# Eight weight tiles made 32 bytes longer in a hybrid decoder layer

## The chip, the cores and the metric

The kernel runs on one core of a Trainium2 chip. The metric is the device time of one execution in microseconds; the median of three executions before the change is 2016.8 us.

## What is computed

One decoder layer over 256 tokens of width 2048, all in float32: a feed-forward block (SwiGLU, inner width 5632), a mixer, a second feed-forward block, and a last RMS norm. Cut to what matters here:

```python
x = x + 0.5 * _swiglu(_rmsnorm(x, n1), w_gate1, w_up1, w_down1)
x = x + _mixer(_rmsnorm(x, nm), ...)      # h @ w_in (2048 x 8208), retention and gated delta heads, mixed @ w_out
x = x + 0.5 * _swiglu(_rmsnorm(x, n2), w_gate2, w_up2, w_down2)
return _rmsnorm(x, nf)
```

The weights (some 376 MB) are each used once, for all 256 tokens.

## The kernel before

**A product.** Every large product keeps the tokens as the stationary operand (a 128 x 128 piece of the activations, loaded into TensorE) and streams the weights as the moving operand, 128 x 512 at a time, into a PSUM accumulator for 128 tokens x 512 output columns. To keep float32 accuracy each operand is split into a high and a low part in the type float32r, and three matmuls are made of each pair (`triple`, lines 149 to 151): high activations with high weights (`whi`), high activations with low weights (`wlo`), low activations with high weights. The three come back to back, so while one matmul streams, the stationary operand of the next one is loaded (the rows called PEld).

**The weights' way.** `weight_piece` (lines 128 to 137) brings one piece, two blocks of 128 rows x 512 columns, so 4096 bytes on each of the 128 partitions: SyncE issues a DMA into `raw` (line 131), ScalarE rounds it into `whi` (line 135), VectorE writes the rest into `wlo` (line 136). A piece then serves 12 matmuls (2 row blocks, 2 token tiles, 3 matmuls). `Stream.take` asks for pieces some places ahead in a plan written out beforehand. The pool `wraw` has four buffers of `raw`; the pool `wsp` has four of `whi` and four of `wlo`, which are used in turn. Only the last four pieces of the whole program go to another pool, `pools["last"]`, which the change leaves as it is. The piece `wab` of the mixer's gates brings its own tile.

**The stages and their stationary operands**, in order of time. The last column counts the matmuls of lines 149 to 151.

| stage | product | stationary tiles | matmuls |
|---|---|---|---|
| first feed-forward | gate and up | `xh`, `xl` | 2112 |
| first feed-forward | down | `hh`, `hl` | 1056 |
| mixer | input, `w_in` | `xh`, `xl` | 1536 |
| mixer | output, `w_out` | `mh..`, `ml..`, `m8` | 384 |
| second feed-forward | gate and up | `xh`, `xl` | 2112 |
| second feed-forward | down | `hh`, `hl` | 1056 |

Each feed-forward block runs in two halves, gate and up of a half and then down of that half, so its two rows of the table alternate. In the mixer the matmuls of `w_in` are interleaved, by a count written in the code (`advance`, one step for each matmul triple), with the steps of the head computations.

**Where the tiles lie.** Tiles stand one behind the other in each partition. An address here is the place of a tile's first byte in its partition, as the built program has it, modulo 256 bytes. A row block of a stationary tile begins a multiple of 512 bytes behind the tile's start, the second row block of a weight piece 2048 bytes behind the first, so the address of a whole tile modulo 256 is that of each operand in it.

| tiles | before | after |
|---|---|---|
| `whi` of `wsp`, buffers 0 to 3 | 160, 160, 160, 160 | 160, 192, 224, 0 |
| `wlo` of `wsp`, buffers 0 to 3 | 160, 160, 160, 160 | 32, 64, 96, 128 |
| `whi`, `wlo` of the last four pieces | 160 | 160 |
| `raw` | 160 | 160 |
| `xh`, `xl` | 160 | 160 |
| `hh`, `hl` in the first feed-forward block | 0 | 0 |
| `hh`, `hl` in the second feed-forward block | 160 | 160 |
| `mh..`, `ml..`, `m8` | 0 | 0 |
| `gu` (moving) and `slr` (stationary) of line 735, in the mixer | 0 and 224 | 0 and 224 |

The distance of two addresses, below, is the moving operand's less that of the stationary operand which is loaded while it streams, modulo 256. Before, it is 0 in every stage whose stationary tiles are at 160, and 160 in the first block's down product and in `w_out`.

Of the kernel before, what the change touches and what calls it, by code (L numbers as in the profile page):

```python
# [14 lines left out]
F32R = mybir.dt.float32r  # L15
# [4 lines left out]
P = 128  # L20
# [5 lines left out]
NB = 512  # L26
# [61 lines left out]
def hybrid_layer(ctx: ExitStack, tc: tile.TileContext, a: dict, out: bass.AP):  # L88
# [8 lines left out]
    wsp = ctx.enter_context(tc.tile_pool(name="wsp", bufs=4))  # L97
# [30 lines left out]
    def weight_piece(src, k, n, pool=wsp, both=None):  # L128

        raw = wraw.tile([P, k, n], F32, name="raw")  # L130
        nc.sync.dma_start(raw, src)
        if both is None:
            both = pool.tile([P, k, n], F32R, name="whi"), pool.tile([P, k, n], F32R, name="wlo")
        hi, lo = both
        S.copy(hi, raw)  # L135
        V.tensor_tensor(lo, raw, hi.bitcast(F32), ALU.subtract)  # L136
        return hi, lo
# [24 lines left out]
    class Stream:  # L162
# [9 lines left out]
        def take(self, w, n):  # L172
            while self.at < len(self.plan) and len(self.ready) <= self.lead:
                name, src, k, pool = self.plan[self.at]
                self.ready.append((name, k, weight_piece(src, k, NB, pools[pool] if pool else wsp)))
                self.at += 1
            name, k, parts = self.ready.popleft()
            assert (name, k) == (w, n)
            return parts
# [289 lines left out]
    with tc.tile_pool(name="gd", bufs=1) as gd:  # L469
        def mixed_out(o, b, xt=None):  # L470
            for t in range(NT):
                xs = x[:, t, b * NB:(b + 1) * NB]
                V.tensor_tensor(xs, o[t], xs, ALU.add)
            later.extend(norm_block(ssqs[2], 2, b, xt))

        env = dict(x_left=x_left, ident=ident, mx=mx, product=product, product_units=product_units, power=power,
                   vector_transposed=vector_transposed, split=split,
                   weight_piece=weight_piece, do_later=do_later, mixed_out=mixed_out,
                   row_factor=lambda: row_factor(ssqs[1]), params=(cst, alog, dtb, gnw, cw, posi))
        mixer(tc, a, gd, env)  # L480
# [605 lines left out]
```

## Time and profile before

| | |
|---|---|
| median of three runs | 2016.8 us (2014.28 to 2017.02) |
| the profiled execution's own time | 2015.32 us |
| its span, first to last instruction | 2013.5 us |
| mean granted TensorE clock | 0.993 of full speed |
| TensorE busy with matmuls | 98% of the span |
| VectorE, ScalarE, GpSimd busy | 65%, 44%, 4% |
| mean busy share of the DMA engines, by slice | mostly 0.5 to 0.6 |

How to read it: the matmuls are pipelined, and a row's duration reaches from a matmul's start to its modelled end, which lies behind the start of the next. So busy time says little on the rate; the distance between the starts of two matmuls that follow each other does, here called the spacing. In a window full of equal matmuls it is the window's length plus one duration, divided by the count (a window counts each matmul that touches it).

### The profile page before, as it was taken

Reading aid. Unit: us, or ns where it says so; the run is one execution under the profiler, and the core shown is the slowest. Engines: PE = TensorE matmul, PEld = TensorE weight load, DVE = VectorE, ACT = ScalarE, POOL = GpSimd, SP = SyncE. Lnnn points to the kernel's source line nnn. Section 1 sums busy time; section 2 is a strip of 40 time slices with the busy share of each in tenths; the row PEclk is TensorE's granted clock in tenths of the full one; section 3 lists DMA queues with packets and bytes.
Section 4 is the critical chain, followed back from the end, with each engine's and each line's share of the span. In section 5 each row is a group of like instructions: output and inputs, shape, how many; then the busy total and the mean of one; then the engine's idle time right before and its main releaser. Section 6 shows DMA issues by size and latency. Waiting matters only on the chain.

```text
span 2013.5 us, 23688 instructions
## 1 busy us (share of the span) xinstructions
PE 1974.1 (98%) x8804; PEld 1617.5 (80%) x8804; DVE 1315.8 (65%) x1878; ACT 890.9 (44%) x1076; POOL 86.9 (4%) x121
## 2 busy tenths in 40 slices
PE   9999999999999999998998999999999999999998
PEld 7888888888888888866877778888888888888886
DVE  6776664457666766564896697766676554667654
ACT  6434443343444446633643344444444434444443
POOL 0000000000000000220132100000000000000000
PEclk9999999999999999998998999999999999999999
DMA  8655655565565566797468555666665556655564
GB/s 302 202 185 188 208 190 188 188 191 186 188 208 189 183 188 181 153 207 161 145 180 200 124 158 184 215 192 194 194 193 187 200 195 192 195 192 188 184 208 142
DMA packets 197604, 379.91 MB, mean 189 GB/s; under 512 B 15280, under 2 KB 15920, under 8 KB 197360
## 3 DMA queue, kind: packets, MB, share of 16 engines
q1 hardware_dynamic: 193888, 368.40, 59.5%
q0 software_dynamic: 3168, 8.65, 1.7%
q8 instruction: 69, 1.13, 0.2%
q10 hardware_dynamic: 432, 1.34, 0.2%
q14 instruction: 47, 0.39, 0.1%
HBM read 375.98 MB, written 2.36 MB: 188 GB/s over the span
## 4 chain that ended last, share of the span: by engine, by line
PE 85%; DVE 5%; DMA 4%; issue 4%; POOL 1%; ACT 1%; DVEq 0%; POOLq 0%; ACTq 0%
PE acc L149 28%; PE acc L151 27%; PE acc L150 27%; DMA nr<-nd 2%; DVE wlo L136 2%; DMA raw<-in_w_in_dram 1%; PE mx L791 1%; DVE mt L254 0%; PE mx L713 0%; DMA nd<-Nd 0%; DVE yn L825 0%; ACT whi L135 0%; DVE Yd L826 0%; POOL nr L810 0%; DVE ht L254 0%
## 5 line engine op out<-in xcount | busy, mean ns | idle before, releaser
L136 DVE TENSOR_TENSOR wlo<-raw,whi 128x1024 fp32r<-128x1024 f32 (+1 forms) x689 | 838.7, 1225 | 557.4 <-ACT whi L135 554.4
L135 ACT CAST whi<-raw 128x1024 fp32r<-128x1024 f32 (+1 forms) x689 | 719.3, 1050 | 859.4 <-PE acc L151 738.6
L149 PE MATMUL acc<-whi,xh 128*128 128x512 f32 x1920 | 760.5, 396 | 1.4 <-DVE xl L269 1.3
L150 PE MATMUL acc<-wlo,xh 128*128 128x512 f32 x1920 | 751.5, 391 | 6.7 <-DVE wlo L136 6.7
L151 PE MATMUL acc<-whi,xl 128*128 128x512 f32 x1920 | 750.8, 391 | 0.0
L150 PEld LDWEIGHTS acc<-wlo,xh 128*128 128x128 f32 x1920 | 362.1, 189 | 81.7 <-DVE wlo L136 10.8
L149 PEld LDWEIGHTS acc<-whi,xh 128*128 128x128 f32 x1920 | 362.1, 189 | 75.7 <-ACT whi L135 3.4
L151 PEld LDWEIGHTS acc<-whi,xl 128*128 128x128 f32 x1920 | 361.8, 188 | 75.4
L149 PE MATMUL acc<-whi,hh 128*128 128x512 f32 x704 | 276.5, 393 | 0.0
L150 PE MATMUL acc<-wlo,hh 128*128 128x512 f32 x704 | 276.5, 393 | 0.0
L151 PE MATMUL acc<-whi,hl 128*128 128x512 f32 x704 | 276.5, 393 | 0.0
L254 DVE STREAM_TRANSPOSE ht<-h 32x256 f32<-32x256 f32 x352 | 153.3, 436 | 5.3
L150 PEld LDWEIGHTS acc<-wlo,hh 128*128 128x128 f32 x704 | 132.4, 188 | 30.0
L151 PEld LDWEIGHTS acc<-whi,hl 128*128 128x128 f32 x704 | 132.4, 188 | 29.9
L149 PEld LDWEIGHTS acc<-whi,hh 128*128 128x128 f32 x704 | 132.4, 188 | 29.8
L141 ACT CAST hh<-ht 128x512 fp32r<-128x512 f32 x44 | 27.2, 618 | 121.3 <-DVE ht L254 121.3
L298 POOL TENSOR_TENSOR rfac<-rms,cexpn 128x2 f32<-128x2 f32 (+1 forms) x5 | 3.2, 642 | 866.0 <-DVE rms L304 866.0
L142 DVE TENSOR_TENSOR hl<-ht,hh 128x512 fp32r<-128x512 f32 x44 | 30.3, 688 | 14.5 <-ACT hh L141 14.4
L345 ACT ACTIVATE sg<-acc,rfac 128x512 f32<-128x512 f32 x44 | 29.9, 689 | 20.2 <-PE acc L151 17.4
L149 PE MATMUL acc<-whi,mh 128*128 128x512 f32 x96 | 38.1, 396 | 0.0
L151 PE MATMUL acc<-whi,ml 128*128 128x512 f32 x96 | 38.1, 396 | 0.0
L150 PE MATMUL acc<-wlo,mh 128*128 128x512 f32 x96 | 38.0, 396 | 0.0
(205 smaller groups left out, 843.8 us busy)
## 6 DMA issues: line engine op xcount, KB each, us to landing
raw<-in_ffn_w_up_dram SPq DMA_DIRECT2D x176, 512.0 KB, 4.4
raw<-in_ffn_w_down_dram SPq DMA_DIRECT2D x176, 512.0 KB, 4.4
raw<-in_ffn_w_gate_dram SPq DMA_DIRECT2D x175, 512.0 KB, 4.4
raw<-in_w_in_dram SPq DMA_DIRECT2D x128, 512.0 KB, 4.8
raw<-in_w_out_dram SPq DMA_DIRECT2D x32, 512.0 KB, 4.3
nr<-nd POOLq DMA_DIRECT2D x64, 128.0 KB, 7.7
x<-in_x_dram SPq DMA_DIRECT2D x4, 512.0 KB, 6.8
out_dram<-x SPq DMA_DIRECT2D x8, 256.0 KB, 2.4
```

The lines of the kernel that those rows point to most:

```text
L135: S.copy(hi, raw)
L136: V.tensor_tensor(lo, raw, hi.bitcast(F32), ALU.subtract)
L141: S.copy(hi, src)
L142: V.tensor_tensor(lo, src, hi.bitcast(F32), ALU.subtract)
L149: PE.matmul(o, lhsT=sh, rhs=hi, start=first, stop=False)
L150: PE.matmul(o, lhsT=sh, rhs=lo, start=False, stop=False)
L151: PE.matmul(o, lhsT=sl, rhs=hi, start=False, stop=last)
L254: V.transpose(dv[q:q + Q, :, :, r:r + Q], sv[r:r + Q, :, :, q:q + Q])
L298: G.tensor_tensor(dst, src, cexp[e][:, 0:1].broadcast_to([P, w]), ALU.pow)
L345: S.activation(sg[:, t, :], g[t], AF.Silu, scale=rf[:, t:t + 1])
L791: PE.matmul(pt[:m, i, :], lhsT=lhsT, rhs=rhs, start=True, stop=True)
```

## The change

Each of the eight tiles of the pool `wsp` gets 8 more float32 elements behind its 1024, which no instruction reads or writes. So each tile begins 32 bytes further on, modulo 256, than the one before it. Eight times 32 is 256, so all tiles behind the pool move by 256 bytes and keep their addresses modulo 256. Line numbers behind the change grow by two. The instructions, their engines, their order, their sizes, buffers and waits stay the same on all five queues; only the addresses in them differ.

```diff
         if both is None:
-            both = pool.tile([P, k, n], F32R, name="whi"), pool.tile([P, k, n], F32R, name="wlo")
+
+            both = [pool.tile([P, 2 * NB + (8 if pool is wsp else 0)], F32R, name=name)[:, :k * n]
+                    .rearrange("p (k n) -> p k n", n=n) for name in ("whi", "wlo")]
         hi, lo = both
```

## Rows read from the trace of the kernel before

**Rows 1.** The page's head and its busy time by engine.
```profile
span 2013.5 us, 23688 instructions
...
PE 1974.1 (98%) x8804; PEld 1617.5 (80%) x8804; DVE 1315.8 (65%) x1878; ACT 890.9 (44%) x1076; POOL 86.9 (4%) x121
```

**Rows 2.** The page's chain of work that ended last, by engine and line.
```profile
PE 85%; DVE 5%; DMA 4%; issue 4%; POOL 1%; ACT 1%; DVEq 0%; POOLq 0%; ACTq 0%
PE acc L149 28%; PE acc L151 27%; PE acc L150 27%; DMA nr<-nd 2%; DVE wlo L136 2%; DMA raw<-in_w_in_dram 1%; PE mx L791 1%; DVE mt L254 0%; PE mx L713 0%; DMA nd<-Nd 0%; DVE yn L825 0%; ACT whi L135 0%; DVE Yd L826 0%; POOL nr L810 0%; DVE ht L254 0%
```

**Rows 3.** The page's costliest groups: busy us, mean ns, idle before.
```profile
L136 DVE TENSOR_TENSOR wlo<-raw,whi 128x1024 fp32r<-128x1024 f32 (+1 forms) x689 | 838.7, 1225 | 557.4 <-ACT whi L135 554.4
L135 ACT CAST whi<-raw 128x1024 fp32r<-128x1024 f32 (+1 forms) x689 | 719.3, 1050 | 859.4 <-PE acc L151 738.6
L149 PE MATMUL acc<-whi,xh 128*128 128x512 f32 x1920 | 760.5, 396 | 1.4 <-DVE xl L269 1.3
...
L150 PE MATMUL acc<-wlo,xh 128*128 128x512 f32 x1920 | 751.5, 391 | 6.7 <-DVE wlo L136 6.7
...
L149 PE MATMUL acc<-whi,hh 128*128 128x512 f32 x704 | 276.5, 393 | 0.0
```

**Rows 4.** Windows of single stages: length, busy us and count by engine.
```profile
core 0: us, PE busy (x) PEld busy (x) DVE busy (x) ACT busy (x) POOL busy (x), PEclk, DMA share, GB/s
...
60.00:270.00 210.00, 209.24 (x923) 172.84 (x922) 139.16 (x176) 92.04 (x99) 0.00 (x0) 1.00 0.62 196
280.00:400.00 120.00, 120.00 (x514) 96.48 (x513) 59.65 (x56) 46.39 (x46) 0.00 (x0) 1.00 0.56 188
405.00:620.00 215.00, 215.00 (x950) 178.00 (x949) 134.83 (x161) 92.89 (x97) 0.00 (x0) 1.00 0.61 193
...
740.00:1190.00 450.00, 423.92 (x2025) 345.15 (x2024) 309.17 (x604) 207.41 (x303) 82.16 (x110) 0.97 0.68 166
1200.00:1280.00 80.00, 80.00 (x343) 64.33 (x342) 67.03 (x105) 36.46 (x49) 0.00 (x0) 1.00 0.54 184
...
1600.00:1700.00 100.00, 100.00 (x443) 82.81 (x442) 48.92 (x43) 39.08 (x38) 0.00 (x0) 1.00 0.59 195
```

**Rows 5.** Groups by line, windows 280 to 400 and 1290 to 2000 us.
```profile
L149 PE MATMUL acc<-whi,hh 128*128 128x512 f32 x171 | 67.8, 396 | 0.0
...
L149 PE MATMUL acc<-whi,hh 128*128 128x512 f32 x346 | 134.6, 389 | 0.0
```

**Rows 6.** Timeline of PE behind the first down product: start us, duration us.
```profile
404.88 0.39 PE L151 MATMUL acc<-whi,hl 128*128 128x512 f32 x1
...
406.96 0.39 PE L151 MATMUL acc<-whi,xl 128*128 128x512 f32 x1
```

**Rows 7.** Timeline of PE behind a late weight load, gate and up.
```profile
54.54 0.39 PE L151 MATMUL acc<-whi,xl 128*128 128x512 f32 x1
...
56.62 0.39 PE L151 MATMUL acc<-whi,xl 128*128 128x512 f32 x1
```

**Rows 8.** Timeline of PE around two matmuls of line 735, mixer.
```profile
996.48 0.39 PE L149 MATMUL acc<-whi,xh 128*128 128x512 f32 x1
996.71 0.62 PE L735 MATMUL mx<-gu,slr 128*128 128x512 f32 x2
997.17 0.39 PE L150 MATMUL acc<-wlo,xh 128*128 128x512 f32 x1
...
998.33 0.39 PE L149 MATMUL acc<-whi,xh 128*128 128x512 f32 x1
```

**Rows 9.** Chain of work within 740 to 1190 us, and within 0 to 60 us.
```profile
by line: PE acc L149 14.1%; PE acc L151 12.8%; PE acc L150 12.7%; DMA nr<-nd 10.7%; DVE wlo L136 8.0%; issue 6.4%; DMA raw<-in_w_in_dram 5.4%; PE mx L791 3.3%; DVE mt L254 2.2%; PE mx L713 2.2%; DMA nd<-Nd 2.0%; DVE yn L825 2.0%; DVE Yd L82
...
by line: issue 85.2%; DVE wlo L136 6.0%; DVE ht L254 4.2%; ACT whi L135 1.8%; POOL rfac L298 1.2%; ACT sg L345 0.5%; DVE ang L666 0.5%; DVE h L349 0.1%; POOLq L298 0.0%; DVEq L136 0.0%; POOLq L1069 0.0%; POOLq L802 0.0%; ACTq L135 0.0%
```

## The prediction

> **What bounds the kernel now.** I read the page's head first: TensorE is busy 1974.1 of 2013.5 us, VectorE 65%, ScalarE 44% [rows 1]. The chain of work that ended last says the same in another way: 82% of it is three lines, the three matmuls of a split product, and everything else together is 18% [rows 2]. So the end is set by how closely these matmuls follow each other, and a change that moves only addresses can act only through that spacing, or through the two engines that fill the changed tiles.
>
> The second view is therefore the windows of single stages [rows 4]. [...] With the window plus one duration over the count: 1600 to 1700 us gives (100 + 0.389) / 443 = 226.6 ns, 405 to 620 us gives 226.7, 60 to 270 us (with its 0.76 us of idle taken off) 227.1; but 280 to 400 us gives (120 + 0.396) / 514 = 234.2, and 1200 to 1280 us 234.4. The three fast windows are products with `xh`, `xl` or the second block's `hh`, `hl`; the two slow ones are the first block's down product and `w_out`. Instructions and shapes are equal in all. The durations repeat it for one and the same line and product: `acc<-whi,hh` lasts 396 ns in the first feed-forward block and 389 in the second [rows 5]. What differs between these two is the address of `hh`, 0 against 160, while the weights lie at 160 in both. So the trace of before holds two cases of the thing that the change alters: distance 0 costs 226.7 ns, distance 160 costs 234.3, which is 7.6 ns or 3.4% more.
>
> The third view is the timeline at places where the distance or the rhythm has just changed. Behind the first down product, when `xh` comes back, nine spacings take 406.96 - 404.88 = 2.08 us, 231 ns each, and only then come the 226.7 [rows 6]. After a late weight load in a gate and up product, at distance 0 throughout, it is again 2.08 us for nine, 231 ns [rows 7]. So the 226.7 ns is a rhythm into which equal matmuls settle after about ten, and a disturbed row runs at some 231 while it settles. In the mixer two matmuls of another line, with distances 32 and 96, stand in a settled row: the three spacings from 996.48 to 997.17 are 230 ns on average, and the five behind them, at distance 0, are 1.16 us or 232 each [rows 8].
>
> **The change part by part.** It removes and adds no instruction and moves none. Three things could have a price.
>
> First, the fill of the tiles. A piece costs VectorE 1.225 us and ScalarE 1.050 us [rows 3], and PE uses it for 12 spacings, 12 x 226.7 = 2.72 us. VectorE's three addresses of line 136 are all 160 now and differ afterwards; no row shows what a different phase does there. Even a fill of 1.5 times the price, 1.84 us, would lie under the 2.72 us, as VectorE's idle time before this line is 557 us in all [rows 3]. In the mixer, where this line has 8.0% of the chain [rows 9], 5% more would cost 450 x 0.08 x 0.05 = 2 us. I take nothing, with 2 us either way. `raw` keeps its addresses, so the DMAs aren't touched.
>
> Second, the stages that now have distance 0: gate and up in both blocks, `w_in`, and the second down product. Afterwards the four `whi` have distances 0, 32, 64 and 96 there, the four `wlo` 128, 160, 192 and 224. Each triple goes high, low, high, so the distance jumps by 128 between one matmul and the next, and changes by 32 from piece to piece. Only buffer 0 of `whi`, 2/3 x 1/4 = 1/6 of the matmuls, keeps distance 0. The price of a jump is bounded by 226.7 ns (the distance doesn't matter) and 234.3 ns (each distance but 0 is as bad as 160). Between them lie the disturbed rows with 231. A row whose distance jumps all the time can't settle as [rows 6] and [rows 7] do, so it is nearest to the disturbed rows, and some of its distances are of the bad sort: I take 232 ns, a rise of 5.3.
>
> How many of these count: the first block's gate and up have 2112 matmuls, but the chain of the first 60 us is 85.2% issue and not PE [rows 9], so 51 us / 226.7 ns = 225 of them are hidden, and 1887 remain. The second block has 2112 + 1056 less the 48 of the last four pieces, which keep 160: 3120. `w_in` has 1536, and there the three lines make 14.1 + 12.8 + 12.7 = 39.6% of the chain [rows 9]: I count 608, and all 1536 at the upper bound, since PE is busy 423.92 of those 450 us [rows 4]. Sum 5615, times 5.3 ns = 29.8 us.
>
> Third, the stages that have distance 160 now: the first down product (1056) and `w_out` (384). There the distances become those of the tiles themselves, a mixture of all eight. At the same 232 ns these 1440 gain 2.3 ns each, 3.3 us.
>
> The sum is +26.5 us. Against the profiled execution's 2015.3 us (its span of 2013.5 and 1.8 around it) it gives 2041.8; that execution lies 1.5 us below the median, so beside it 2043.3. I say 2043.
>
> [...] The rows: 226.6 and 234.2 ns for the same instruction stream, with nothing different but where the stationary tile lies [rows 4, 5]. [...]
>
> **The rivals.**
>
> No change. The stationary operand's own address could be what decides, 160 good and 0 bad, whatever the moving one's; then all stages keep their spacing and the time is 2015 to 2018 us. For it: in the rows of before the large products' moving tiles never lie anywhere but at 160, so [rows 4, 5] can't part the two readings. [...] Against it: in [rows 8] the stationary operand behind the second `gu` matmul is at 160 as before and only the moving one is elsewhere, and the row is out of its rhythm afterwards, five spacings of 232. Chance 0.09.
>
> Faster. The 7.6 ns could be peculiar to distance 160 and a few others, while most distances are as good as 0. If 160 alone is bad, then in the first group only one `wlo` buffer of four pays, 1/12 of the matmuls, 5615 x 7.6 / 12 = +3.6 us; in the second group only one `whi` buffer still pays, 1/6, and 5/6 are freed: 1440 x 7.6 x 5/6 = -9.1 us. Net -5.5, 2011 us. For it: the first spacing of [rows 8], at distance 192, is 0.23 us, as at rest. Against it: the disturbed rows, which run at 231 without any bad distance [rows 7]. It decides when the first group's mean rises by less than d, where 5615 d = 1440 (7.6 - d): d = 1.6 ns, so below 228.3 ns. Chance 0.11.
>
> Slower, but by half. If what matters repeats every 64 bytes, 160 is the same as 32, and half of the pieces keep the good rhythm: mean 230.5, 5615 x 3.8 = 21.3 less 1440 x 3.8 = 5.5, +16 us, 2033. At the other end each distance but 0 is like 160: 5615 x 7.6 x 5/6 = 35.6, and all of `w_in` counted adds 928 x 6.3 = 5.9, less 1440 x 7.6 / 6 = 1.8 : +40, 2057. These two bound the likeliest case.
>
> **How the numbers follow.** Slower by the mechanism above 0.80, no change 0.09, faster 0.11. The likeliest case's own range is 2030 to 2060. The range given has to hold 8 of 10 with cases of both signs: it goes down to 2014, which takes in the case of no change, and up to 2062, the upper bound with the 2 us of the fill and the 1.5 us of the median, rounded. A change within 0.2%, 4 us, can't be told from none: faster 0.11, same 0.09, slower 0.80.
>
> **What the profile after would show.** Right: in windows of `xh` products (1600 to 1700 us or so) the count falls from 443 to about 433, the mean duration of `acc<-whi,xh` rises from 389 to some 395, PE's granted clock stays at 1.00, PE shows no new idle time, and the window of the first down product shows a few more matmuls than now. Lines 136 and 135 keep 1225 and 1050 ns. Wrong: counts that don't move (the stationary address decides), or that rise in the down product and stay in the others (160 is peculiar), or durations of line 136 that move and come into PE's waits.

## The result, and the profile after

| | before | after |
|---|---|---|
| median | 2015.66 us (4 runs, 2014.28 to 2017.02) | 2043.12 us (4 runs, 2040.85 to 2043.77) |
| span of the profiled execution | 2013.5 us | 2039.0 us |

The ratio is 1.0136, with a 95% interval from 1.0124 to 1.0148: the change costs 27 us. The two profiled executions, 2015.32 and 2040.85 us, differ by 25.5 us, and it is this difference that the traces can account for.

The page of the changed kernel: its head, busy time by engine, the chain that ended last, and the costliest groups that answer to [rows 3].

```profile
span 2039.0 us, 23688 instructions
...
PE 2006.4 (98%) x8804; PEld 1622.0 (80%) x8804; DVE 1318.1 (65%) x1878; ACT 889.0 (44%) x1076; POOL 86.8 (4%) x121
...
PE 88%; DVE 4%; issue 4%; DMA 3%; ACT 1%; POOL 1%; POOLq 0%; DVEq 0%; ACTq 0%
...
L138 DVE TENSOR_TENSOR wlo<-raw,whi 128x1024 fp32r<-128x1024 f32 (+1 forms) x689 | 840.9, 1226 | 584.0 <-ACT whi L137 578.6
L137 ACT CAST whi<-raw 128x1024 fp32r<-128x1024 f32 (+1 forms) x689 | 716.9, 1046 | 891.5 <-PE acc L153 793.9
L151 PE MATMUL acc<-whi,xh 128*128 128x512 f32 x1920 | 770.9, 402 | 1.6 <-DVE xl L271 1.6
```

The same work is done; the two engines that fill the padded tiles keep their price (1226 and 1046 ns against 1225 and 1050 in [rows 3]), and `acc<-whi,xh` lasts 402 ns on average where it lasted 396. The windows say where. They are those of [rows 4], with the same columns:

```profile
60.00:270.00 210.00, 209.79 (x904) 169.53 (x903) 137.78 (x175) 90.58 (x98) 0.00 (x0) 1.00 0.61 192
280.00:400.00 120.00, 120.00 (x519) 97.06 (x518) 63.47 (x65) 46.06 (x46) 0.00 (x0) 1.00 0.56 189
405.00:620.00 215.00, 215.00 (x928) 174.09 (x927) 132.87 (x159) 90.84 (x96) 0.00 (x0) 1.00 0.60 189
740.00:1190.00 450.00, 429.85 (x2034) 347.59 (x2033) 310.07 (x589) 208.70 (x305) 82.45 (x112) 0.98 0.69 170
1200.00:1280.00 80.00, 80.00 (x346) 64.68 (x346) 65.85 (x99) 38.85 (x54) 0.00 (x0) 1.00 0.56 190
1600.00:1700.00 100.00, 100.00 (x432) 80.97 (x431) 47.40 (x43) 37.77 (x36) 0.00 (x0) 1.00 0.58 190
```

The granted clock is 1.00 and PE is busy throughout, as before, outside the mixer. 1600 to 1700 us has 432 matmuls for 443, 405 to 620 us 928 for 950: by the window plus one duration over the count 232.4 and 232.1 ns, where it was 226.6 and 226.7. The two slow windows have become a little faster: 519 for 514 and 346 for 343, so 232.0 and 232.4 ns where it was 234.2 and 234.4. All these stages now run at the same 232.

In PE's timeline of the second block's gate and up the starts lie 0.23 or 0.24 us apart:

```profile
1501.22 0.39 PE L153 MATMUL acc<-whi,xl 128*128 128x512 f32 x1
1501.45 0.39 PE L151 MATMUL acc<-whi,xh 128*128 128x512 f32 x1
1501.68 0.40 PE L152 MATMUL acc<-wlo,xh 128*128 128x512 f32 x1
1501.91 0.40 PE L153 MATMUL acc<-whi,xl 128*128 128x512 f32 x1
1502.15 0.39 PE L151 MATMUL acc<-whi,xh 128*128 128x512 f32 x1
```

These few rows, told to 0.01 us, can't part one step from several. The whole second half of the first block's gate and up can, 960 matmuls from 410.43 us on: the pieces in the four buffers take, in turn, 233.1, 230.3, 232.5 and 233.1 ns a matmul on average, where all four took 226.7 before.

### The profile page after: what moved, and what is told of

It reads as the page before. It is cut to its first block, busy times and chain, and to the rows that moved or that the text cites. A ratio compares the mean times of both kernels' runs of the same rounds, so it can differ in the third digit from the quotient of the medians.

```text
span 2039.0 us, 23688 instructions
## 1 busy us (share of the span) xinstructions
PE 2006.4 (98%) x8804; PEld 1622.0 (80%) x8804; DVE 1318.1 (65%) x1878; ACT 889.0 (44%) x1076; POOL 86.8 (4%) x121
## 4 chain that ended last, share of the span: by engine, by line
PE 88%; DVE 4%; issue 4%; DMA 3%; ACT 1%; POOL 1%; POOLq 0%; DVEq 0%; ACTq 0%
PE acc L151 28%; PE acc L152 28%; PE acc L153 28%; DVE wlo L138 2%; DMA raw<-in_w_in_dram 2%; DMA nr<-nd 2%; PE mx L793 1%; DVE mt L256 0%; PE mx L715 0%; ACT whi L137 0%; PE mx L774 0%; DVE ht L256 0%; DVE yn L827 0%; PE mx L688 0%; DVE Yd L828 0%
## 5 line engine op out<-in xcount | busy, mean ns | idle before, releaser
L138 DVE TENSOR_TENSOR wlo<-raw,whi 128x1024 fp32r<-128x1024 f32 (+1 forms) x689 | 840.9, 1226 | 584.0 <-ACT whi L137 578.6
L137 ACT CAST whi<-raw 128x1024 fp32r<-128x1024 f32 (+1 forms) x689 | 716.9, 1046 | 891.5 <-PE acc L153 793.9
L151 PE MATMUL acc<-whi,xh 128*128 128x512 f32 x1920 | 770.9, 402 | 1.6 <-DVE xl L271 1.6
L152 PE MATMUL acc<-wlo,xh 128*128 128x512 f32 x1920 | 760.9, 396 | 3.5 <-DVE wlo L138 3.5
L153 PE MATMUL acc<-whi,xl 128*128 128x512 f32 x1920 | 760.7, 396 | 0.0
```

Of the source, the lines that this page charges most:

```text
L151: PE.matmul(o, lhsT=sh, rhs=hi, start=first, stop=False)
L152: PE.matmul(o, lhsT=sh, rhs=lo, start=False, stop=False)
L153: PE.matmul(o, lhsT=sl, rhs=hi, start=False, stop=last)
```

## The experiments

Twelve kernels ran, eleven made from the kernel before and one from the changed kernel. All but one ran once, beside the kernel before on the same chip (2014.9 to 2018.1 us). Nine runs of the kernel before on one of these chips went from 2013.83 to 2016.96 us, so differences of 2 or 3 us between single runs say little. In the tables, "x stages" are those whose stationary tiles lie at 160 before, and "down and out" the first block's down product and `w_out`. The spacings are worked out as above from the windows 405 to 620 us (x stages) and 280 to 400 us (first down product). In the slower kernels the first down product still runs at 405 us; where it has another spacing than the x stages, the window 1310 to 1525 us, all gate and up, is the clean one.

### A constant distance

Is it the jump of the address from one matmul to the next that costs, or the distance itself? Four kernels move all eight weight tiles together, by 32, 64, 96 or 128 bytes, and leave everything else where it was modulo 256. For 32:

```diff
+    ctx.enter_context(tc.tile_pool(name="pad0", bufs=1)).tile([P, 8], F32, name="pad0")
     wsp = ctx.enter_context(tc.tile_pool(name="wsp", bufs=4))
+    ctx.enter_context(tc.tile_pool(name="pad1", bufs=1)).tile([P, 56], F32, name="pad1")
```

Moved by 32: 

> All eight weight tiles at 192, so no jumps: the distance is 32 throughout in the stages with stationary tiles at 160, and 192 in the first down product and the mixer's output product. Theory A (it is the jumping distance that costs, a constant one settles): the spacing settles to one repeating pattern from 226 to 234 ns, below the 232.2 and 233.2 ns that these distances show in the changed kernel; 2005 to 2035 us. Theory B (each distance has its price whether it jumps or not): 232.2 and 233.2 ns as in the changed kernel, about 2045 us. Theory C (the stationary address alone decides): 226.7 and 234.3 ns as before, 2015 us.

Moved by 64: 

> All eight weight tiles at 224: distance 64 constant where the stationary tiles are at 160, 224 in the first down product and the mixer's output product. Theory A (jumps cost): a settled spacing below the 229.8 and 232.7 ns of the changed kernel, 226 to 230; 2005 to 2030 us. Theory B (each distance has its price): 229.8 and 232.7 ns, about 2031 us. Theory C (stationary address alone): 226.7 and 234.3 ns, 2015 us.

Moved by 96: 

> All eight weight tiles at 0: distance 96 constant where the stationary tiles are at 160, and 0 in the first down product and the mixer's output product, so the good case changes sides. Theory A (jumps cost, the distance decides the settled rhythm): 226.7 ns in the first down product; at 96, unseen without jumps, 227 to 234 ns; 2005 to 2048 us. Theory B (each distance has its price): 232.8 ns at distance 0 and 234.0 at 96 as in the changed kernel, 2055 us. Theory C (stationary address alone): 226.7 ns where the stationary tile is at 160 and 234.3 in the first down product, 2015 us.

Moved by 128: 

> All eight weight tiles at 32: distance 128 constant where the stationary tiles are at 160, and 32 in the first down product and the mixer's output product. Theory A (jumps cost): settled spacings from 226 to 234 ns, that at 32 equal to the one which the kernel with the tiles at 192 shows for distance 32 in its other stages; 2005 to 2055 us. Theory B (each distance has its price): 234.0 and 230.0 ns, about 2050 us. Theory C (stationary address alone): 226.7 and 234.3 ns, 2015 us.

The windows of the kernel moved by 64:

```profile
280.00:400.00 120.00, 120.00 (x516) 96.61 (x515) 61.35 (x61) 45.55 (x46) 0.00 (x0) 1.00 0.59 188
405.00:620.00 215.00, 215.00 (x940) 176.37 (x940) 133.84 (x160) 92.06 (x97) 0.00 (x0) 1.00 0.64 191
1310.00:1525.00 215.00, 215.00 (x941) 176.42 (x940) 139.62 (x179) 91.10 (x97) 0.70 (x1) 1.00 0.64 190
```

of the one moved by 96:

```profile
280.00:400.00 120.00, 120.00 (x531) 99.33 (x530) 65.54 (x69) 47.17 (x47) 0.00 (x0) 1.00 0.61 193
405.00:620.00 215.00, 215.00 (x924) 173.05 (x923) 132.88 (x159) 90.06 (x96) 0.00 (x0) 1.00 0.63 189
1310.00:1525.00 215.00, 215.00 (x923) 172.95 (x922) 136.82 (x172) 89.53 (x95) 0.70 (x1) 1.00 0.64 190
```

and of the one moved by 128:

```profile
405.00:620.00 215.00, 215.00 (x927) 174.29 (x926) 133.11 (x160) 90.56 (x95) 0.00 (x0) 1.00 0.64 189
1310.00:1525.00 215.00, 215.00 (x923) 173.02 (x922) 133.48 (x162) 90.43 (x95) 0.70 (x1) 1.00 0.63 190
```

The kernel before ran beside these four in 2017.51 us.

| tiles moved by | x stages: distance, ns | down and out: distance, ns | time, us |
|---|---|---|---|
| 0 (before) | 0, 226.7 | 160, 234.2 | 2015.66 |
| 32 | 32, 233.4 | 192, 233.3 | 2050.44 |
| 64 | 64, 228.9 | 224, 233.3 | 2027.28 |
| 96 | 96, 233.4 | 0, 226.7 | 2041.97 |
| 128 | 128, 232.4 up to the mixer, 233.4 behind it | 32, 233.3 | 2048.74 |

The kernel moved by 96 decides against theory C: the first down product runs at 226.7 ns with its stationary tiles where they always were, at 0, because the weights are now at 0 too; and the x stages lose their 226.7. It is the pair of addresses that counts. Distance 32 gives the same 233.3 to 233.4 in two different stages. So a constant distance is dear without any jump: 64 costs 2.2 ns, each of the other six 5.7 to 7.5. Theory A in its pure form (a constant distance settles cheaply) falls with the kernels moved by 32, 96 and 128. As recorded it allowed up to 234 ns at 96 and 128, so of its numbers only those for the kernel moved by 32 (233.4 ns, expected below 232.2; 2050 us, expected 2035 at most) and for distance 224 (233.3, expected below 232.7) clearly fail. Theory B misses in the other direction, since distance 0 costs 226.7 here where theory B had 232.8 from the changed kernel, and 64 costs 228.9 (expected 229.8).

### A jump, with good distances

Three kernels split the padding's pattern: `whi` stays at 160 and only `wlo` moves, by 128 or by 64; or `whi` and `wlo` of a buffer lie at the same address, which goes on by 32 from buffer to buffer. Two pools take the place of `wsp`, with the unused bytes between and behind them, and `weight_piece` takes `wlo` from the second; for the steps each tile has 8 more elements. For 128, cut to the pools:

```diff
     wsp = ctx.enter_context(tc.tile_pool(name="wsp", bufs=4))
+    ctx.enter_context(tc.tile_pool(name="pad1", bufs=1)).tile([P, 32], F32, name="pad1")
+    wlop = ctx.enter_context(tc.tile_pool(name="wlop", bufs=4))
+    ctx.enter_context(tc.tile_pool(name="pad2", bufs=1)).tile([P, 32], F32, name="pad2")
```

Low tiles by 128: 

> The high tiles stay at 160, the four low tiles lie at 32, nothing changes from piece to piece: where the stationary tiles are at 160 the distance is 0, 128, 0 within each triple. Theory A (the jump itself keeps the row from settling): about 232 ns, +28 us, 2045 us. Theory B (each matmul pays the constant price of its distance, 226.7 at 0 and 232.8 at 128): (2 x 226.7 + 232.8) / 3 = 228.7 ns, +11 us, 2028 us.

Low tiles by 64: 

> As the kernel with the jump of 128, but with the low tiles at 224: distance 0, 64, 0 where the stationary tiles are at 160; 160, 224, 160 in the first down product and the mixer's output product. Theory A (the jump itself costs): about 232 ns, 2040 to 2045 us. Theory B (constant price of each distance, 226.7 at 0 and 229.0 at 64): 227.5 ns, +4 us, 2021 us.

Steps: 

> High and low tile of one buffer at the same address, and 32 bytes further with each buffer: no jump within a piece of 12 matmuls, one step of 32 from piece to piece, distances 0, 32, 64, 96 where the stationary tiles are at 160. Theory A (jumps cost; a row needs about ten matmuls to settle): near 231 to 232 ns, for there is no time to settle; +24 to +30 us, about 2043 us. Theory B (constant price of each distance): (226.7 + 233.3 + 229.0 + 233.3) / 4 = 230.6 ns, less 3 us in the other stages, +18 us, 2035 us.

Measured: 2038.09, 2048.82 and 2038.16 us. The low tiles moved by 64:

```profile
280.00:400.00 120.00, 120.00 (x511) 95.88 (x510) 62.84 (x66) 45.87 (x45) 0.00 (x0) 1.00 0.58 185
405.00:620.00 215.00, 215.00 (x928) 173.90 (x927) 132.85 (x159) 91.02 (x96) 0.00 (x0) 1.00 0.64 189
```

From 405 us on 928 matmuls, 232.1 ns, as many as in the changed kernel, with no distance in these stages but 0 and 64, of which the one costs 226.7 and the other 228.9 when constant. Here the jump alone is the price, and theory B's 227.5 is off by 4.6. The first down product, with distances 160, 224, 160, runs at 235.6, above the 234.2 and 233.3 of these two when constant; by that this kernel's time lies 4 us above theory A's range too. The steps give 930 in the same window, 231.6 ns, where theory B had 230.6 and theory A 231 to 232; theory A's time was 5 us too long, theory B's 3 us too short. The low tiles moved by 128 don't give one number, and their time is neither theory's:

```profile
280.00:400.00 120.00, 120.00 (x521) 97.45 (x520) 61.77 (x60) 46.06 (x45) 0.00 (x0) 1.00 0.59 191
405.00:620.00 215.00, 215.00 (x941) 176.08 (x940) 134.06 (x161) 91.70 (x97) 0.00 (x0) 1.00 0.64 192
1310.00:1525.00 215.00, 215.00 (x923) 173.03 (x922) 138.12 (x176) 88.67 (x94) 0.70 (x1) 1.00 0.63 186
```

The last two windows are gate and up products with the same addresses; the earlier runs at 228.9 ns, theory B's price, the later at 233.4, above theory A's. One order of addresses has two rhythms here. And the first down product, with distances 160, 32, 160, runs at 231.1 ns, below the 234.2 and 233.3 of these two when constant: here a jump between bad distances gained.

### Every large product at distance 0

```diff
     posi = par.tile([P, NT], mybir.dt.int32, name="posi")
+    par.tile([P, 40], F32, name="pad")
```

The pool `par` stands ahead of the first block's and the mixer's tiles and is closed before the second block's.

> The kernel before with 160 unused bytes ahead of the first feed-forward block's and the mixer's tiles, so that these stationary tiles lie at 160 like the weights: distance 0 in every large product. Theories A and B: 226.7 ns in the first down product and the mixer's output product too, 1440 x 7.5 ns = 10.8 us less than before, about 2005 us. If the loss of these two products has another cause than the distance: no change, 2016 us.

Measured, as medians of five runs and of nine of the kernel before: 2006.98 us against 2015.82, ratio 0.9957, 95% interval 0.9943 to 0.997. It is the fastest version of the study.

```profile
280.00:400.00 120.00, 120.00 (x531) 99.36 (x530) 61.50 (x58) 48.11 (x47) 0.00 (x0) 1.00 0.62 193
405.00:620.00 215.00, 215.00 (x950) 178.05 (x949) 135.07 (x161) 92.56 (x98) 0.00 (x0) 1.00 0.65 193
740.00:1190.00 450.00, 422.54 (x2010) 344.53 (x2009) 311.58 (x609) 206.46 (x300) 82.11 (x110) 0.97 0.68 166
1200.00:1280.00 80.00, 79.91 (x353) 65.50 (x351) 67.86 (x104) 39.97 (x55) 0.00 (x0) 1.00 0.57 182
```

The first down product has 531 matmuls for 514 in [rows 4], 226.7 ns, and `w_out` 353 for 343: both gain as expected. The mixer gives about 2 of the 11 us back: its window has 2010 matmuls for 2025, and from the start of `w_in` to that of `w_out` it takes 461.9 us for 460.3. All tiles of the head computations have moved too there, by 160 bytes; whether one of them costs this, or it is the scatter from one execution to the next, was not tried.

### Half the load

Does the loss come from the load of the next stationary tile, which runs while the weights stream? Two kernels, from before and from the changed kernel, load 64 of the 128 columns in all but the first and the last row block of a product. So half of those matmuls' results is left out, and each of them also writes 64 rows of the accumulator for 128:

```diff
+        if not (first or last):
+            o, sh, sl = o[:HALF], sh[:, :HALF], sl[:, :HALF]
         PE.matmul(o, lhsT=sh, rhs=hi, start=first, stop=False)
```

Without the padding: 

> The kernel before, but the stationary operand has only 64 of its 128 columns in all but the first and the last row block of each product, so half of the accumulation is left out; the moving stream keeps its 512 columns, its addresses and its order. Theory L (the loss comes from the load of the next stationary tile, which reads while the weights stream): with half the load, the spacing falls below 226.7 ns in the stages with distance 0, to 216 to 222 ns, and the first down product falls below 234.3; 1930 to 1990 us. Theory M (the moving stream's own addresses or rate set the spacing): 226.7 and 234.3 ns as before, 2015 us.

With it: 

> The changed kernel with the same half load. Theory L (the load of the next stationary tile is what collides): what the padding adds shrinks with the load, from 5.4 ns to about 3 or less where the stationary tiles are at 160; 10 to 17 us more than the half load without the padding. Theory M (the moving stream alone): the padding costs its full 5.4 ns, 25 us or more over the half load without it.

Measured: 2021.11 us without the padding and 2036.35 with it. A load in the kernel before, and then the half load without the padding:

```profile
200.13 0.19 PEld L150 LDWEIGHTS acc<-wlo,xh 128*128 128x128 f32 x1
...
200.06 0.13 PEld L153 LDWEIGHTS acc<-whi,xl 128*64 128x64 f32 x1
...
280.00:400.00 120.00, 120.00 (x524) 72.30 (x523) 63.03 (x64) 46.84 (x46) 0.00 (x0) 1.00 0.60 190
405.00:620.00 215.00, 215.00 (x938) 132.08 (x937) 134.00 (x160) 91.55 (x97) 0.00 (x0) 1.00 0.64 191
```

and with it:

```profile
405.00:620.00 215.00, 215.00 (x933) 131.45 (x932) 133.80 (x160) 91.08 (x96) 0.00 (x0) 1.00 0.64 191
```

A load is shorter, 0.13 us for 0.19, but at distance 0 the spacing rises, to 229.6 ns, and at 160 it falls, to 229.8 (a mean over a row that doesn't settle: groups of 60 matmuls in this stage take 226.7 to 231.8). With the padding it is 230.9, so the padding adds 1.3 ns instead of 5.4, as theory L had it (3 or less). That it adds 15 us, inside L's 10 to 17, is in good part luck: by the stages' starts 9 of them fall into `w_in`, which takes 454.6 us without the padding and 463.8 with it, and only 6 into the other large products. And L's main figure, 216 to 222 ns, is clearly wrong, as is M's (226.7 and 234.3 unchanged). The stationary side has a part in the rhythm, for halving it moves both spacings and nearly removes the difference between them (0.2 ns where it was 7.5); whether by the load or by the halved output these two runs can't part. The loss is not proportional to the load's length: the load keeps 0.13 of its 0.19 us, the padding's price 1.3 of its 5.4 ns.

### The tile being loaded

While one matmul streams, the tile of the next is loaded: in the kernel before, line 149's matmul starts at 200.12 us, the load for line 150 runs from 200.13 to 200.32, and line 150's matmul starts at 200.35. In the last pair the low activations `xl` (and `hl` of the second block) move by 128, once together with the low weights, so that stream and load always have the same address, once alone. Cut to `xl`:

```diff
+    keep.tile([P, 32], F32, name="padx")
     xl = keep.tile([P, KD, T], F32R, name="xl")
+    keep.tile([P, 32], F32, name="pady")
```

Together: 

> High weights at 160 and low weights at 32 as in the kernel with the jump of 128, and the low activations (xl in both blocks and the mixer, hl in the second block) at 32 too. A low weight tile streams while the low activations of the next matmul are loaded, so the distance to the tile being loaded is 0 at every matmul although the moving address jumps by 128; the distance to the matmul's own stationary tile is 0, 128, 128. Theory N (what counts is the distance between the stream and the load that runs beside it): 226.7 ns again in these stages, 2011 to 2017 us. Theory O (the distance to the own stationary tile) and theory J (the jump of the moving address by itself): 231 to 233 ns, 2035 to 2045 us.

Alone: 

> All weights at 160 as before, only the low activations (xl, and hl in the second block) at 32: the moving address never jumps, the distance to the tile being loaded is 0, 128, 0. Theory N (the distance between the stream and the load beside it, and its changes): as with the jump of 128 in the weights, 231 to 232 ns in the stages with stationary tiles at 160, 2035 to 2043 us. Theory J (only a jump of the moving address): 226.7 ns, 2016 us.

Measured: 2033.91 and 2041.35 us. The windows 405 to 620 us, together and then alone:

```profile
405.00:620.00 215.00, 215.00 (x932) 174.68 (x931) 133.63 (x160) 91.05 (x96) 0.00 (x0) 1.00 0.64 190
```

```profile
405.00:620.00 215.00, 215.00 (x932) 175.86 (x931) 133.01 (x160) 91.71 (x96) 0.00 (x0) 1.00 0.64 189
```

Both 932, 231.1 ns. Theory N falls with the first: equal addresses of stream and load don't bring the 226.7 back when both jump. Theory J falls with the second: the weights never move there, only the loaded tile does, and the price is the same. Theory O, the distance to the tile that the matmul itself uses, had 231 to 233 ns for the first and gets it, with a time 1 us below its range; no run sets it against a jump of the loaded tile, so it is not excluded. What is left is that a row at distance 0 lost its 226.7 when the moving part jumped (232.1, low tiles by 64) and when the stationary part did (231.1, `xl` alone).

## Why the prediction was right

**The step that carries it held.** The prediction took 232 ns for every stage after the change, "nearest to the disturbed rows, and some of its distances are of the bad sort". The windows after give 232.0 to 232.4. Both halves of the reason are now shown apart: a jump between distances that are good by themselves costs 4.6 ns over their constant prices (low tiles by 64), and the bad sort is six of the eight distances and not just 160 (the four moved kernels). The changed kernel has both; with the constant prices of its distances its x stages would come to 2/3 x (226.7 + 233.4 + 228.9 + 233.4) / 4 + 1/3 x (232.4 + 234.2 + 233.3 + 233.3) / 4 = 231.5 ns, where 232.1 is measured. So in its mean the jumps add only 0.6 ns, and the bad distances alone would nearly have given the time. The prediction's reason, that a row which jumps all the time stays near 231, is not the whole: jumps cost at good distances, and between bad ones the first down product gained (231.1, low tiles by 128) or lost (235.6, low tiles by 64). Its upper bound of 234.3 is no bound either, by that 235.6. That it all ends so near to 232 could not be seen from the rows of before; it was a choice inside bounds, and it fell well.

**The sum, term by term,** from the start of each stage's first matmul in the timelines of both kernels (us, the second half of a stage added to its first):

| stage | predicted | measured |
|---|---|---|
| gate and up, first block | +10.0 | +11.5 |
| down, first block | -2.4 | -2.1 |
| mixer, `w_in` | +3.2 | -0.7 |
| mixer, `w_out` | -0.9 | -0.8 |
| second block | +16.5 | +17.3 |
| sum | +26.5 | +25.2 |

The term that was mis-sized is `w_in`. It was counted with 608 of its 1536 matmuls, by PE's share of the chain. Its matmuls do run slower: where two of them follow each other without a wait, they start 228.1 ns apart on average before and 232.0 after. But the stage takes no longer, 460.3 us before and 459.6 after, by its first matmul and the first of `w_out`, before and then after:

```profile
735.20 0.39 PE L149 MATMUL acc<-whi,xh 128*128 128x512 f32 x1
...
1195.48 0.39 PE L149 MATMUL acc<-whi,m 128*128 128x512 f32 x1
```

```profile
744.87 0.40 PE L151 MATMUL acc<-whi,xh 128*128 128x512 f32 x1
...
1204.49 0.40 PE L151 MATMUL acc<-whi,m 128*128 128x512 f32 x1
```

PE's idle time in the window 740 to 1190 us took it up: 450 - 423.92 = 26.1 us in [rows 4], 20.2 after. That is one execution of each; in the eight other kernels with whole loads whose gate and up products run at 231 ns or more in one block or both, the stage takes 460.6 to 463.3 us, so 0.3 to 3.0 more than before. The chain's share says how often PE was the last to end, and not what a slower PE adds where the chain also holds VectorE (`wlo` 8.0% in [rows 9], 6.6% after) and DMAs (`nr<-nd` 10.7% and 7.1%, `raw` 5.4% and 7.5%); which of them took the slack up was not tried.

Against it stands the first block's gate and up with 1.5 us more than predicted. The 225 matmuls that the prediction counted as hidden behind the "issue" of the first 60 us weren't, for that stretch of the chain grew itself, by 1.5 us (before, then after; start and length in us):

```profile
0.79 48.27 issue
```

```profile
0.79 49.80 issue
```

All 2112 matmuls at 5.4 ns come to 11.4 us, and 11.5 is measured. One reading of the prediction is loose, without weight in the sum: 1600 to 1700 us is no window of `xh` products but mostly of the second block's down product, which is at distance 0 as well. That the median falls on the 2043 of the prediction to the microsecond is luck: the misses in the terms partly cancel, and the 1.5 us that it added for the median were 0.3 before and 2.3 after.

**The fill** was costed at nothing, and is: 1226 and 1046 ns on average, with seven of the eight tiles at new addresses.

**The rivals.** "No change", by the stationary address alone, is out by the kernel moved by 96. "Faster", with 160 as a peculiar distance, is out by the kernels moved by 32, 96 and 128; the first group's mean would have had to stay below 228.3 ns, and it is 232. A repeat every 64 bytes is out as well: 64 and 128 give 228.9 and 232.4 where 0 gives 226.7. In steps of 32 bytes the runs show no repeat shorter than 256; that 256 is the period was not tried, it is only the measure in which the addresses are told here.

**What stays open** is the mechanism. Shown is that the spacing depends on the pair of moving and stationary addresses, told modulo 256 (226.7 to 234.2 ns with the same instructions), that jumps of either spoil it at distance 0 (232.1 and 231.1), and that the stationary side's size takes part (229.6 and 229.8 with half of its columns). Not shown is what in TensorE makes the difference, nor which of the successive reads has to agree with which: neither "stream and load" (theory N) nor "stream alone" (theories J and M) explains all runs, the loss isn't proportional to the load (theory L), and the matmul's own tile (theory O) stays possible. Nor is it shown why a jump between bad distances gains in one kernel and costs in another.

## What to carry to other kernels

Look at the spacing of starts, stage by stage, before calling a kernel bound by TensorE finished: equal matmuls at 226.7 ns in one stage and 234.2 in another were a placement here, and 160 unused bytes ahead of the slow stages' tiles were worth 9 us. What was fastest here, at 2006.98 us, had the buffers through which the weights rotate, and the stationary tiles that they meet, at one address modulo 256; the padding that spread them gave 2043.12. A gain or loss on the busiest engine still has to be followed stage by stage: where it waits for a chain anyway, it can come out as idle time and not in the end, as in `w_in`, with 20.2 us idle for 26.1 and 459.6 us in all for 460.3.

## What the runs showed of the hardware that was not expected

One order of addresses had two rhythms here: the kernel with the low tiles moved by 128 ran its gate and up products at 228.9 ns up to the mixer and at 233.4 behind it, with the clock granted in full in both windows, and the kernel with all tiles moved by 128 had 232.4 and 233.4 in the same way. What chose the rhythm was not tried. So a short stretch of such a kernel needn't stand for the whole.

Several of the spacings lie on a ladder. 226.7 (before), 228.9 (all tiles by 64), 231.1 (`xl` by 128) and 233.4 ns (all tiles by 96), each the mean of a window of 215 us, are some 2.2 ns apart, so that a triple of matmuls takes about 680, 687, 693 or 700 ns; the 235.6 of the first down product with the low tiles moved by 64 would be the next rung. Others lie between the rungs: 234.2 in the first down product before (234.2 or 234.3 in each group of 60 matmuls), 232.1 with the low tiles moved by 64. What sets them was not tried.
